# A two-layer decoder trunk: layer 0 reads raw tokens, its memory attention moves between recurrence groups, values go out 512 columns at a time, and the recurrence carries a state

## The chip, the cores and the metric

One core of one Trainium2 chip runs the whole program. The metric is the device time of one execution in microseconds (us), as a median of several runs. The engines named below are TensorE (PE, with PEld for its weight loads), VectorE (DVE), ScalarE (ACT), GpSimd (POOL) and SyncE (SP), whose queue issues the DMAs. TensorE has two clock levels, 1.2 and 2.4 GHz; a profile gives the granted share of the higher one.

## The reference, cut to what is touched

512 tokens of width 1024 pass through two layers. Layer 0 mixes tokens by a gated linear recurrence (6 heads, key and value width 128), layer 1 by latent attention; in both, a 4-head cross-attention over 256 memory rows runs beside the mixer, and a gated MLP with a 3-tap convolution follows.

```python
h = rms_norm(x, mix_norm_g[0])
z = h @ hg_w_in                       # columns [q 768 | f 768 | i 768 | g 768 | memory query 256]
q = silu(q) * 128**-0.5; fg = lb + (1-lb)*sigmoid(f); k = 1-fg; logf = log(fg); v = i
# per head, over time, b = cumulative sum of logf:
#   o[t] = sum over s<=t of (q[t] . exp(b[t]-b[s]) k[s]) v[s]
#   the reference does it in chunks with a state:
state = state * exp(b_last)[..., None] + einsum('bhsk,bhsv->bhkv', k*exp(b_last-b), v)
y = rms_norm(o, onorm_g) * silu(g)
m = memory_attention(z[..., -256:], rms_norm(mem, mem_norm_g[0]), w_mem_kv[0], ...)
x = x + concatenate([y, m]) @ w_out[0]
```

## The kernel before

**Tiling.** Activations lie transposed, eight tiles of 128 channels by 512 tokens. Each matrix product runs in three matmuls (`mm3`, L173): operands are split into a high part (`whi`, `xh`, fp32r, by ACT) and a rest (`wlo`, `xl`, by DVE), and hi·hi, hi·lo and lo·hi are summed in PSUM. Weights come by DMA in chunks of up to 128x1024 (`chunk`, L220): three `raw` buffers, two `whi` and two `wlo`. `gemm` (L242) has two forms: weights stationary and 512 tokens moving, which gives 128 channels by 512 tokens; or `tokens=True`, 128 tokens stationary and the weight's columns moving. Products inside the recurrence and the attention's values are plain fp32 and not split; each such matmul leaves two records in the trace, a transpose leaves one.

**PSUM.** Eight banks: four `acc`, two `at`, two `tp`.

**Order.** Program order is a priority, not an order of issue: when the program is built, a planner lays out each engine's queue, taking whatever is ready by its own estimate, earlier instructions first. On the chip each engine then works its own queue strictly in order. So work written later fills gaps of work written earlier, as far as buffers are free.

**Layer 0 before.** First the parameters, the memory (`mt`, 2 DMAs of 512 KB), two memory weights and the tokens (`xt`, 4 DMAs) are issued on SP. The memory rows are transposed, split (`turn`, L318) and projected (`project`, L332; 48 matmuls of 512 columns). The tokens' squares give the norm, `xn` is the scaled token (L546), 32 transposes turn it (L550) and `split` writes `nh`/`nl` (L551). Memory queries (L557; 96 matmuls of 256 columns) follow, then 32 more transposes of the raw `xt` (L561) for the residual `X`, whose second half of tokens is kept reversed (L562, L563). Then both pairs of memory heads (`attend`, L398) and the recurrence.

**The recurrence** works on three groups of two heads, in the order of `SCAN` (L82): F (forget gate), Q, G (output gate), V (values, 256 columns, L621), L (`levels`, L631) and N (`finish`, L695). `levels` doubles the block length nine times: at levels 0 to 6 it multiplies keys and queries inside windows of 128 tokens (ACT copies `kp`, PE two matmuls, DVE a predicated copy into `Ad` and three multiplies, for each of two heads); levels 7 and 8 (L671 to L680) give the products between different windows, copied by ACT to `Ao`. `finish` multiplies `Ad` and `Ao` by the values (L700 to L704), then normalizes: squares, a product with ones, an inverse root of 12 small DVE instructions, four transposes, a multiply and a split. The two heads share one buffer each for `osq` and `oy`. `kq` has two buffers for each of `Dg`, `Kc` and `Qc`. Then `out_proj` (L449): two groups, each with four `acc` banks and chunks in the order [6,7] (memory heads), [0,1], [2,3], [4,5].

**Layer 1** uses the same `Memory` class, in the order `PRE` (L80), where u is `turn` and p `project`.

Of the kernel before, what the change touches and what calls it, by code (L numbers as in the profile page):

```python
# [8 lines left out]
F32 = mybir.dt.float32  # L9
# [33 lines left out]
OFF = {0: (0, 128, 384), 1: (384, 256, 256), 3: (640, 256, 128)}  # L43
# [7 lines left out]
def _span(a, n):  # L51
    return [(a, a + n)]


def _weights():
    w = {}
    w["hg_w_in"] = (("hg_w_in", 0), [
        (_span(o + 256 * b, 256), QUADS) for b in range(3) for o in (768, 0, 1536, 2304)] + [(_span(3072, 256), QUADS)])
# [21 lines left out]
PRE = "a L b n u c p m d q k r"  # L80

SCAN = "F0 Q0 G0 L0 V0 F1 Q1 L1 N0 V1 G1 F2 Q2 N1 L2 V2 G2 N2"  # L82
# [14 lines left out]
def hybrid_trunk_kernel(ctx, tc, x, mem, params, pos, wts, out, tap):  # L97
# [208 lines left out]
    class Memory:  # L306
        def __init__(self, layer, pool):
            self.layer = layer
# [4 lines left out]
        def load(self, pool):  # L313
            self.mt = [pool.tile([P, D], F32, name=f"mt{b}") for b in range(2)]
            for b in range(2):
                nc.sync.dma_start(self.mt[b], mem[b * P:(b + 1) * P, :])

        def turn(self, pool):  # L318
            self.mth = [pool.tile([P, MEM], F32R, name=f"mth{d}") for d in range(KD)]
            self.mtl = [pool.tile([P, MEM], F32R, name=f"mtl{d}") for d in range(KD)]  # L320
            for d2 in range(KD // 2):
                ps = tp_tile()
                for d in range(2):
                    for b in range(2):
                        c = (2 * d2 + d) * P
                        transpose(ps[:, d * MEM + b * P:d * MEM + (b + 1) * P], self.mt[b][:, c:c + P])
                for d in range(2):
                    k = 2 * d2 + d
                    split(self.mth[k], self.mtl[k], ps[:, d * MEM:(d + 1) * MEM],
                          scale=pcol("memg", self.layer * KD + k, 1))  # L330

        def project(self):  # L332
            self.pk = [acc_tile(), acc_tile()]
            for c, kts in enumerate(PAIRS):
                hi, lo = chunk(f"w_mem_kv{self.layer}", 0, c)
                for j, kt in enumerate(kts):
                    for b in range(2):
                        r = slice(b * P, (b + 1) * P)
                        mm3(self.pk[b], self.mth[kt][:, r], self.mtl[kt][:, r], hi[:, j, :], lo[:, j, :],
                            kt == 0, kt == KD - 1)  # L340

        def keys(self, pool):
            layer, pk = self.layer, self.pk
            kv = pool.tile([P, 2, MW], F32, name="kv")
            kvf = pool.tile([P, D], F32, name="kvf")
            mss = sm.tile([P, 2], F32, name="mss")
            for b in range(2):
                act(kvf, self.mt[b], AF.Square, accum_out=mss[:, b:b + 1])
            rm = sm.tile([P, 2], F32, name="rm")
            rsqrt(rm, mss, D)  # L350
            for b in range(2):
                act(kv[:, b, :], pk[b][:, 0:MW], AF.Identity, scale=rm[:, b:b + 1])
                act(self.v[:, b, :], pk[b][:, MW:], AF.Identity, scale=rm[:, b:b + 1])
# [3 lines left out]
            kk = pool.tile([P, 2, MW], F32, name="kk")  # L357
            act(kk, kv[:, :, 0:MW], AF.Square)
# [15 lines left out]
        def queries(self, wname, group, xh, xl, tok, slot):  # L374
            self.qm = [slot(9 + i, F32) for i in range(2)]

            def evac(t, ps):
                dst = self.qm[t // 2][:, (t % 2) * MW:(t % 2 + 1) * MW]
                if tok is None:
                    act(dst, ps, AF.Copy)  # L380
                else:
                    act(dst, ps, AF.Identity, scale=tok[:, t:t + 1])

            gemm(wname, group, xh, xl, evac, tokens=True)
# [135 lines left out]
    with ExitStack() as l0:  # L520
# [4 lines left out]
        with tc.tile_pool(name="load", bufs=1) as lp, tc.tile_pool(name="mem0", bufs=1) as mp:  # L525
            memory = Memory(0, mp)
            with tc.tile_pool(name="mkt0", bufs=1) as mk:
                nc.sync.dma_start(par[:, :48], params[:, :48])
                memory.load(mk)
                for c in range(2):  # L530
                    chunk("w_mem_kv0", 0, c, ahead=True)
                xt = [lp.tile([P, D], F32, name=f"xt{t}") for t in range(NT)]
                for t in range(NT):
                    nc.sync.dma_start(xt[t], x[t * P:(t + 1) * P, :])
                nc.sync.dma_start(par[:, 48:], params[:, 48:])
                memory.turn(mk)
                memory.project()
                xn = []
                for t in range(NT):
                    xn.append(kq.tile([P, D], F32, name="xn", tag="Kc" if t < 2 else "Qc"))  # L540
                    junk = kq.tile([P, D], F32, name="junk", tag="Dg")
                    xss = sm.tile([P, 1], F32, name="xss")
                    act(junk, xt[t], AF.Square, accum_out=xss)
                    xr = sm.tile([P, 1], F32, name="xr")
                    rsqrt(xr, xss, D)
                    ts(xn[t], xt[t], xr, None, ALU.mult)  # L546
                for d in range(KD):
                    ps = tp_tile() if d % 2 else at_tile()
                    for t in range(NT):
                        transpose(ps[:, t * P:(t + 1) * P], xn[t][:, d * P:(d + 1) * P])  # L550
                    split(nh[d], nl[d], ps, scale=pcol("mixg", d, 1))  # L551
                memory.keys(mk)
            with tc.tile_pool(name="mat", bufs=1, reuse_waits="tile") as mat:
                def slot(i, dtype, n=1):
                    return mat.tile([P, S] if n == 1 else [P, n, S], dtype, name=f"slot{i}")

                memory.queries("hg_w_in", 12, nh, nl, None, slot)  # L557
                for d in range(KD):
                    ps = tp_tile()
                    for t in range(NT):  # L560
                        transpose(ps[:, t * P:(t + 1) * P], xt[t][:, d * P:(d + 1) * P])  # L561
                    nc.vector.tensor_copy(out=X[:, d, :H], in_=ps[:, :H])  # L562
                    nc.vector.tensor_copy(out=X[:, d, H:], in_=ps[:, :H - 1:-1])  # L563
                memory.norms(slot)
                memory.attend((0, 1), slot, yh, yl)
# [27 lines left out]
        with tc.tile_pool(name="scan", bufs=1, reuse_waits="tile") as sp:  # L593
            for k in range(HH):
                yh[k] = sp.tile([P, S], F32R, name=f"yh{k}")
                yl[k] = sp.tile([P, S], F32R, name=f"yl{k}")
            def silu2(ps, dst):

                act(dst, ps, AF.Tanh, scale=0.5)
                stt(dst, dst, 1.0, ps, ALU.add, ALU.mult)  # L600

            def forget(b):
# [3 lines left out]
                def ev_f(m, ps):  # L606
                    h = 2 * b + m
                    z = kq.tile([P, S], F32, name="z")
                    act(z, ps, AF.Tanh, scale=0.5)
# [3 lines left out]
                gemm("hg_w_in", 4 * b, nh, nl, ev_f)  # L613
                return Dg, Kc

            def query(b):
                Qc = kq.tile([P, 2, S], F32, name="Qc")
                gemm("hg_w_in", 4 * b + 1, nh, nl, lambda m, ps: silu2(ps, Qc[:, m, :]))
                return Qc

            def value(b):  # L621
                V = sp.tile([P, NT, 256], F32, name="V", bufs=2)
                gemm("hg_w_in", 4 * b + 2, nh, nl, lambda t, ps: act(V[:, t, :], ps, AF.Copy), tokens=True)
                return V

            def gate(b):
                Gt = sp.tile([P, 2, S], F32, name="Gt", bufs=2)
                gemm("hg_w_in", 4 * b + 3, nh, nl, lambda m, ps: silu2(ps, Gt[:, m, :]))
                return Gt

            def levels(b, Dg, Kc, Qc):  # L631

                Ad = sp.tile([P, 2, NT, P], F32, name="Ad", bufs=2)
                Ao = [sp.tile([P, 768], F32, name=f"Ao{h}", bufs=2) for h in range(2)]
                dcur = [Dg[:, h, :] for h in range(2)]

                def put(h, sb, t, src):

                    c = OFF[sb][0] + t - OFF[sb][1]
                    act(Ao[h][:, c:c + src.free_size()], src, AF.Copy)  # L640
# [9 lines left out]
                for lv in range(9):  # L650
                    m = 1 << lv
                    for h in range(2):
                        Kf, Qf = Kc[:, h, :], Qc[:, h, :]
                        ps = at_tile()
                        if lv < 8:
                            kv, qv = blocks(Kf, m, 0), blocks(Qf, m, 1)
                        if lv < 7:
                            nb = 64 // m
                            kp = kq.tile([P, H], F32, name=f"kp{h}", bufs=1)

                            act(kp.rearrange("p (b two j) -> p b two j", two=2, j=m),
                                bass.AP(tensor=kv.tensor, offset=kv.offset,
# [393 lines left out]
```

## Time and profile before

| what | us |
|---|---|
| median of 3 runs | 1253.29 |
| lowest, highest | 1253.13, 1253.79 |
| the profiled execution's own time | 1253.92 |
| its span, first to last instruction | 1251.9 |
| PE busy, DVE busy, ACT busy | 1229.0, 754.6, 561.4 |
| mean granted clock of TensorE | 0.998 of 2.4 GHz |

Busy is the union of an engine's instructions; a matmul's end is modelled and matmuls overlap, so a matmul's price is read from the distance of two starts, not from its duration. Layer 0's mixer takes the span up to about 300 us, its MLP up to about 660, layer 1's mixer up to about 860, its MLP the rest.

### The profile page before, as it was taken

How to read it: one execution, taken by the hardware profiler on the slowest of the kernel's cores; microseconds unless marked ns; L12 is line 12 of the kernel's file. 1: busy time of each engine (PE TensorE's matmuls, PEld its weight loads, DVE VectorE, ACT ScalarE, POOL GpSimd, SP SyncE). 2: the span in 40 equal slices, each digit the busy share in tenths (PEclk: the TensorE clock that was granted, in tenths of full speed). 3: DMA queues.
4: the chain of work that ended last, by engine and by line, in shares of the span. 5: the costliest groups of instructions: out<-in, count | busy, mean ns of one | idle time of the engine just before them, and what ended most of it. 6: DMA issues, size and time to landing. Idle time of an engine off the chain costs nothing.

```text
span 1251.9 us, 15952 instructions
## 1 busy us (share of the span) xinstructions
PE 1229.0 (98%) x6100; PEld 1022.4 (82%) x6100; DVE 754.6 (60%) x1536; ACT 561.4 (45%) x978; POOL 19.3 (2%) x50
## 2 busy tenths in 40 slices
PE   6999999999999999999999999999999999999998
PEld 4879888988888888888889878777888888888887
DVE  7857575665676757651425758774666766764222
ACT  6464444433443534432325689754453444443211
POOL 6000000000000000000000000000000000000000
PEclk9999999999999999999999999999999999999999
DMA  6212212122222232322323312101223233332331
GB/s 247 70 52 58 78 52 84 51 68 101 101 92 95 100 102 88 99 99 102 101 78 116 104 49 74 35 34 63 90 84 102 85 101 101 99 96 92 116 119 51
DMA packets 31756, 110.44 MB, mean 88 GB/s; under 512 B 3777, under 2 KB 4161, under 8 KB 31681
## 3 DMA queue, kind: packets, MB, share of 16 engines
q1 hardware_dynamic: 31680, 109.43, 26.5%
q8 instruction: 48, 0.79, 0.3%
q14 instruction: 28, 0.22, 0.1%
HBM read 107.32 MB, written 2.10 MB: 87 GB/s over the span
## 4 chain that ended last, share of the span: by engine, by line
PE 92%; ACT 4%; DVE 2%; issue 1%; DMA 1%; SPq 0%; DVEq 0%; ACTq 0%
PE acc L171 63%; PE at L171 24%; PE tp L202 3%; PE tp L171 3%; ACT xl L191 1%; ACT whi L191 0%; DVE wlo L179 0%; ACT pr L191 0%; ACT kv L191 0%; DMA mt<-in_mem 0%; ACT yl L191 0%; ACT q L191 0%; ACT xh L191 0%; ACT yh L191 0%; DVE Ad L667 0%
## 5 line engine op out<-in xcount | busy, mean ns | idle before, releaser
L179 DVE TENSOR_TENSOR wlo<-raw,whi 128x1024 fp32r<-128x1024 f32 (+2 forms) x201 | 240.3, 1196 | 383.0 <-ACT whi L191 377.4
L191 ACT ACTIVATE whi<-raw 128x1024 fp32r<-128x1024 f32 (+2 forms) x201 | 208.8, 1039 | 464.8 <-PE acc L171 303.7
L171 PE MATMUL acc<-xh,whi 128*128 128x512 f32 x616 | 241.3, 392 | 0.0
L171 PE MATMUL acc<-xh,wlo 128*128 128x512 f32 x616 | 241.2, 392 | 0.0
L171 PE MATMUL acc<-xl,whi 128*128 128x512 f32 x616 | 240.9, 391 | 0.0
L171 PEld LDWEIGHTS acc<-xh,whi 128*128 128x128 f32 x616 | 115.7, 188 | 24.2 <-issue 1.0
L171 PEld LDWEIGHTS acc<-xl,whi 128*128 128x128 f32 x616 | 115.7, 188 | 23.8
L171 PEld LDWEIGHTS acc<-xh,wlo 128*128 128x128 f32 x616 | 115.7, 188 | 23.6
L182 DVE SCALAR_TENSOR_TENSOR t<-u,par,t 128x510 f32<-128x510 f32 (+1 forms) x176 | 121.6, 747 | 4.2 <-ACT t L191 4.2
L171 PE MATMUL at<-xh,wlo 128*128 128x512 f32 x232 | 90.5, 390 | 0.0
L171 PE MATMUL at<-xl,whi 128*128 128x512 f32 x232 | 90.3, 389 | 0.0
L171 PE MATMUL at<-xh,whi 128*128 128x512 f32 x232 | 90.3, 389 | 0.0
L191 ACT ACTIVATE t<-u,par 128x512 f32<-128x512 f32 x88 | 67.0, 808 | 41.7 <-DVE u L179 41.7
L171 PE MATMUL acc<-wlo,xh 128*128 128x256 f32 (+2 forms) x224 | 67.8, 303 | 1.3 <-DVE wlo L179 1.3
L171 PE MATMUL acc<-whi,xh 128*128 128x256 f32 (+2 forms) x224 | 67.9, 305 | 0.5 <-ACT xh L191 0.4
L171 PE MATMUL acc<-whi,xl 128*128 128x256 f32 (+2 forms) x224 | 67.8, 303 | 0.0
L171 PE MATMUL acc<-wlo,ah 128*128 128x512 f32 x132 | 51.4, 389 | 0.0
L171 PE MATMUL acc<-whi,ah 128*128 128x512 f32 x132 | 51.4, 389 | 0.0
L171 PE MATMUL acc<-whi,al 128*128 128x512 f32 x132 | 51.4, 389 | 0.0
L171 PEld LDWEIGHTS at<-xl,whi 128*128 128x128 f32 x232 | 43.5, 188 | 9.1
L171 PEld LDWEIGHTS at<-xh,wlo 128*128 128x128 f32 x232 | 43.6, 188 | 9.0
L171 PEld LDWEIGHTS at<-xh,whi 128*128 128x128 f32 x232 | 43.6, 188 | 9.0
(326 smaller groups left out, 2159.6 us busy)
## 6 DMA issues: line engine op xcount, KB each, us to landing
raw<-in_w_up SPq DMA_DIRECT2D x88, 512.0 KB, 3.4
raw<-in_w_down SPq DMA_DIRECT2D x44, 512.0 KB, 3.5
raw<-in_hg_w_in SPq DMA_DIRECT2D x26, 512.0 KB, 3.6
raw<-in_w_out SPq DMA_DIRECT2D x16, 512.0 KB, 3.5
raw<-in_w_mem_kv SPq DMA_DIRECT2D x8, 512.0 KB, 4.4
mt<-in_mem SPq DMA_DIRECT2D x4, 512.0 KB, 4.9
xt<-in_x SPq DMA_DIRECT2D x4, 512.0 KB, 8.0
out<-u SPq DMA_DIRECT2D x8, 256.0 KB, 2.0
```

The costliest lines, as they stand in the source:

```text
L171: nc.tensor.matmul(ps, a, b, start=start, stop=stop)
L179: nc.vector.tensor_tensor(out=o, in0=a, in1=b, op=op)
L182: nc.vector.scalar_tensor_tensor(out=o, in0=a, scalar=s, in1=b, op0=op0, op1=op1)
L191: nc.scalar.activation(out=o, in_=a, func=f, **kw)
L202: nc.tensor.transpose(out=ps, in_=src, identity=ident)
```

## The change

1. **Start.** The tokens are loaded first; parameters go on ACT's queue; the first two chunks of `hg_w_in` follow the tokens on SP. 32 transposes of the raw tokens fill all eight PSUM banks (four `acc`, two `at`, two `tp`). From these `nh`/`nl` are split with the gain, and `X` is copied, half by ACT and half by DVE. The token's inverse root `tok` is computed beside it and spread over a tile `bc`.
2. **Norm on the products.** F, Q and G multiply each PSUM tile by `bc` on DVE before the tanh; values and memory queries take `tok` as the scale of the ACT copy that they had anyway.
3. **Values.** Two products with 512 columns (values of groups 0 and 1; values of group 2 beside the memory queries), in four chunks of two row tiles, instead of three plus one with 256 columns.
4. **Order.** `SCAN` carries the memory part: Mt (load, transposes, projection), Mk (keys), Mn (norms), M0 and M1 (`attend`). `turn` becomes part of `project`, with two pairs of buffers for the turned memory instead of sixteen tiles. The memory's tiles use the places of `yh`/`yl`, which `outputs()` takes just before the first N. Layer 1 uses the same new `project`.
5. **State.** Levels 7 and 8 and `Ao` go. `levels` keeps the total decay of a window (`tot`) and returns `Kc` and `Qc`, which `finish` now reads. `states` transposes three key windows for each head, copies them by ACT, multiplies them by the values and adds up three states; `finish` multiplies these by the queries.

```diff
-PRE = "a L b n u c p m d q k r"
-SCAN = "F0 Q0 G0 L0 V0 F1 Q1 L1 N0 V1 G1 F2 Q2 N1 L2 V2 G2 N2"
+PRE = "a L b n c p m d q k r"
+SCAN = "F0 Q0 Mt V1 G0 L0 Mk Mn V0 F1 M0 Q1 L1 M1 N0 G1 F2 Q2 N1 L2 G2 N2"
...
         def project(self):
-            self.pk = [acc_tile(), acc_tile()]
+            pk = [acc_tile(), acc_tile()]
             for c, kts in enumerate(PAIRS):
...
+                th = self.place(f"mth{c % 2}", [P, 2, MEM], F32R)
+                tl = self.place(f"mtl{c % 2}", [P, 2, MEM], F32R)
...
+            xt = [lp.tile([P, D], F32, name=f"xt{t}") for t in range(NT)]
+            nc.scalar.dma_start(par[:, :48], params[:, :48])
+            for t in range(NT):
+                nc.sync.dma_start(xt[t], x[t * P:(t + 1) * P, :])
+            for c in range(2):
+                chunk("hg_w_in", 0, c, ahead=True)
+            nc.scalar.dma_start(par[:, 48:], params[:, 48:])
+            ps8 = [acc_tile() for _ in range(4)] + [at_tile() for _ in range(2)] + [tp_tile() for _ in range(2)]
+            xss = sm.tile([P, NT], F32, name="xss", bufs=1)
+            for t in range(NT):
                 for d in range(KD):
+                    transpose(ps8[d][:, t * P:(t + 1) * P], xt[t][:, d * P:(d + 1) * P])
+                junk = kq.tile([P, D], F32, name="junk", tag="Dg")
+                act(junk, xt[t], AF.Square, accum_out=xss[:, t:t + 1])
+            for d in range(KD):
+                split(nh[d], nl[d], ps8[d], scale=pcol("mixg", d, 1))
+                act(X[:, d, :H], ps8[d][:, :H], AF.Copy)
+                nc.vector.tensor_copy(out=X[:, d, H:], in_=ps8[d][:, :H - 1:-1])
+            rsqrt(tok, xss, D)
+            spread(tok, 0, bc)
...
             def silu2(ps, dst):
-                act(dst, ps, AF.Tanh, scale=0.5)
-                stt(dst, dst, 1.0, ps, ALU.add, ALU.mult)
+                z = kq.tile([P, S], F32, name="z")
+                tt(dst, ps, bc, ALU.mult)
+                act(z, dst, AF.Tanh, scale=0.5)
+                stt(dst, z, 1.0, dst, ALU.add, ALU.mult)
...
+                if g == 0:
+                    v4 = sp.tile([P, NT, 512], F32, name="v4")
+                    gemm("hg_w_in", 9, nh, nl, lambda t, ps: act(v4[:, t, :], ps, AF.Identity, scale=tok[:, t:t + 1]), tokens=True)
+                    V[0], V[1] = v4[:, :, :256], v4[:, :, 256:]
...
-                for lv in range(9):
+                for lv in range(7):
...
+            def states(b, Kc, tot, V):
+                St = sp.tile([P, 2, 3, P], F32, name="St", bufs=1)
+                for h in range(2):
+                    c = slice(h * P, (h + 1) * P)
+                    ps = at_tile()
+                    for i in range(3):
+                        w = TIME[i]
+                        transpose(ps[:, i * P:(i + 1) * P], Kc[:, h, w * P:(w + 1) * P])
+                    kt_ = kq.tile([P, 3, P], F32, name="ktok", bufs=1)
+                    act(kt_, ps[:, :3 * P].rearrange("p (i k) -> p i k", k=P), AF.Copy)
+                    up = at_tile()
+                    for i in range(3):
+                        mm(up[:, i * P:(i + 1) * P], kt_[:, i, :], V[:, TIME[i], c], True, True)
+                    act(St[:, h, 0, :], up[:, :P], AF.Copy)
+                    for i in range(1, 3):
+                        w = TIME[i]
+                        stt(St[:, h, i, :], St[:, h, i - 1, :], tot[:, h, w:w + 1], up[:, i * P:(i + 1) * P], ALU.mult, ALU.add)
+                return St
...
-                    for sb in (0, 1, 3, 2):
-                        mm(o[:, sb * P:(sb + 1) * P], V[:, sb, c], Ad[:, h, sb, :], sb == 0, sb == 2)
-                        if sb in OFF:
-                            at, t, n = OFF[sb]
-                            mm(o[:, t:t + n], V[:, sb, c], Ao[h][:, at:at + n], False, False)
+                    for i, w in enumerate(TIME):
+                        r = slice(w * P, (w + 1) * P)
+                        mm(o[:, r], V[:, w, c], Ad[:, h, w, :], i == 0, False)
+                    for i, w in enumerate(TIME[1:]):
+                        r = slice(w * P, (w + 1) * P)
+                        mm(o[:, r], St[:, h, i, :], Qc[:, h, r], False, i == 2)
...
+                    if b == 0:
+                        outputs()
+                    finish(b, *got[f"L{b}"], V[b], got[f"G{b}"])
```

## Rows read from the trace of the kernel before

**Rows 1.** the page's first part: busy time, share of the span and count.

```profile
PE 1229.0 (98%) x6100; PEld 1022.4 (82%) x6100; DVE 754.6 (60%) x1536; ACT 561.4 (45%) x978; POOL 19.3 (2%) x50
```

**Rows 2.** busy time by stretch; the columns are named in the first line.

```profile
core 0: us, PE busy (x) PEld busy (x) DVE busy (x) ACT busy (x) POOL busy (x), PEclk, DMA share, GB/s
0.00:45.30 45.30, 34.21 (x204) 28.59 (x205) 33.86 (x122) 27.09 (x48) 19.29 (x50) 1.00 0.54 195
45.30:98.00 52.70, 52.61 (x277) 38.57 (x276) 31.73 (x79) 28.75 (x64) 0.00 (x0) 1.00 0.19 61
205.00:266.00 61.00, 60.94 (x392) 54.11 (x391) 41.92 (x129) 21.59 (x42) 0.00 (x0) 1.00 0.19 58
300.00:660.00 360.00, 360.00 (x1597) 298.38 (x1596) 208.72 (x279) 139.00 (x173) 0.00 (x0) 1.00 0.29 97
660.00:860.00 200.00, 193.01 (x1108) 160.12 (x1107) 133.41 (x437) 139.40 (x369) 0.00 (x0) 0.99 0.20 63
```

**Rows 3.** timeline of PE, 256-column matmuls: start, us, engine, line, operation, tiles, count.

```profile
35.75 0.28 PE L171 MATMUL acc<-whi,xh 128*128 128x256 f32 x1
...
37.43 0.28 PE L171 MATMUL acc<-whi,xl 128*128 128x256 f32 x1
```

**Rows 4.** timeline of PE, the residual's transposes and the first forget-gate matmul.

```profile
44.52 1.04 PE L202 MATMUL tp<-ident,xt 128*128 128x128 f32 x8
45.31 0.47 PE L171 MATMUL acc<-xh,whi 128*128 128x512 f32 x1
```

**Rows 5.** timeline of PE, one head's last products of the first recurrence group.

```profile
143.94 0.81 PE L171 MATMUL tp<-Ao,V 128*128 128x384 f32 x2
144.59 0.38 PE L171 MATMUL tp<-Ad,V 128*128 128x128 f32 x2
144.81 0.60 PE L171 MATMUL tp<-Ao,V 128*128 128x256 f32 x2
145.24 0.38 PE L171 MATMUL tp<-Ad,V 128*128 128x128 f32 x2
```

**Rows 6.** timeline of PE, the kernel's beginning.

```profile
4.99 0.45 PE L202 MATMUL tp<-ident,mt 128*128 128x128 f32 x1 [4.99 <-DMA mt<-in_mem]
...
6.17 1.76 PE L202 MATMUL tp<-ident,mt 128*128 128x128 f32 x7 [0.73 <-DMA mt<-in_mem]
...
10.20 0.79 PE L171 MATMUL acc<-whi,mth 128*128 128x512 f32 x1 [2.28 <-ACT mth L191]
...
14.97 0.63 PE L171 MATMUL acc<-wlo,mth 128*128 128x512 f32 x1
15.40 0.46 PE L171 MATMUL acc<-whi,mth 128*128 128x512 f32 x1
...
16.60 0.40 PE L171 MATMUL acc<-whi,mtl 128*128 128x512 f32 x1
16.83 0.39 PE L171 MATMUL acc<-whi,mth 128*128 128x512 f32 x1
```

**Rows 7.** timeline of DVE, splits of the normed tokens.

```profile
30.98 0.74 DVE L182 SCALAR_TENSOR_TENSOR xl<-tp,par,xh 128x512 fp32r<-128x512 f32 x1
31.63 0.74 DVE L182 SCALAR_TENSOR_TENSOR xl<-at,par,xh 128x512 fp32r<-128x512 f32 x1
```

**Rows 8.** groups of DVE instructions by form, copies into the residual: count, busy, mean ns.

```profile
L562 DVE COPY X<-tp 128x256 f32<-128x256 f32 x8 | 3.4, 419 | 0.5 <-PE tp L202 0.3
```

**Rows 9.** timeline of DVE, third recurrence group and the end of its heads.

```profile
208.30 0.68 DVE L182 SCALAR_TENSOR_TENSOR Qc<-Qc,acc 128x512 f32<-128x512 f32 x1
...
234.57 1.22 DVE L179 TENSOR_TENSOR wlo<-raw,whi 128x1024 fp32r<-128x1024 f32 x1
...
250.13 0.69 DVE L179 TENSOR_TENSOR oy<-tp,Gt 128x512 f32<-128x512 f32 x1
...
257.30 0.69 DVE L179 TENSOR_TENSOR oy<-tp,Gt 128x512 f32<-128x512 f32 x1 [0.65 <-ACT osq L191]
...
264.12 0.75 DVE L182 SCALAR_TENSOR_TENSOR yl<-oy,ongh,yh 128x512 fp32r<-128x512 f32 x1 [0.79 <-ACT yh L191]
```

More of the change, by code (lines that the diff above doesn't have):

```diff
@@ L311, in __init__, with load, project @@
             self.v = pool.tile([P, 2, MW], F32, name="mv")
-        def load(self, pool):
-            self.mt = [pool.tile([P, D], F32, name=f"mt{b}") for b in range(2)]
+        def load(self):
+            self.mt = self.place("mt", [P, 2, D], F32)
             for b in range(2):
[L316 to L321, printed above, removed]
+                nc.sync.dma_start(self.mt[:, b, :], mem[b * P:(b + 1) * P, :])
+        def project(self):
+            pk = [acc_tile(), acc_tile()]
+            for c, kts in enumerate(PAIRS):
                 ps = tp_tile()
@@ L524, in hybrid_trunk_kernel @@
         yl = {k: yp.tile([P, S], F32R, name=f"yl{k}") for k in (6, 7)}
[L525 to L546, printed above, removed]
-                for d in range(KD):
[L548 to L565, printed above, removed]
@@ L693, in levels @@
-                return Ad, Ao
-            def finish(b, Ad, Ao, V, Gt):
+                        kv, qv = blocks(Kf, m, 0), blocks(Qf, m, 1)
+                        nb = 64 // m
+                        kp = kq.tile([P, H], F32, name=f"kp{h}", bufs=1)
+                        act(kp.rearrange("p (b two j) -> p b two j", two=2, j=m),
+                            bass.AP(tensor=kv.tensor, offset=kv.offset,
+                                    ap=[list(kv.ap[0]), [2 * m, P // m], [H + m, 2], [1, m]]), AF.Copy)
@@ L696, in finish @@
+            def finish(b, Ad, Kc, Qc, tot, V, Gt):
+                St = states(b, Kc, tot, V)
                 for h in range(2):
@@ L719, in hybrid_trunk_kernel @@
             for op in SCAN.split():
-                kind, b = op[0], int(op[1])
+                kind, b = op[0], op[1]
+                if kind == "M":
+                    if b == "t":
+                        memory.load()
+                        memory.project()
+                    elif b == "k":
+                        memory.keys()
+                    elif b == "n":
+                        memory.norms(slot)
+                    else:
+                        memory.attend((int(b),), slot, yh, yl)
+                    continue
+                b = int(b)
                 if kind == "F":
@@ L725, in hybrid_trunk_kernel @@
                 elif kind == "V":
-                    got[op] = value(b)
+                    value(b)
                 elif kind == "G":
@@ L845, in hybrid_trunk_kernel @@
                     "r": krot,
-                    "q": lambda: memory.queries("mla_w_in", 2, norm.h, norm.l, norm.tok, slot),
+                    "q": lambda: (memory.query_tiles(slot), gemm("mla_w_in", 2, norm.h, norm.l, lambda t, ps: memory.put_queries(t, ps, norm.tok), tokens=True)),
                 }
```

165 lines of the change are left out of this document (76 added, 89 removed).

## The prediction

> **What bounds the kernel now.** I read the page's busy shares first [rows 1]: PE is busy 98% of the span, DVE 60%, ACT 45%. A share alone proves little, since matmuls overlap, so the windows by stretch come next [rows 2]. In the MLP of layer 0 PE starts 1597 matmuls in 360.00 us, one every 0.2254 us, with nothing idle; that is the price of a 512-column matmul. From 45.3 us on the mixer of layer 0 is filled too (52.61 of 52.70 us, 60.94 of 61.00). Only two places have holes: the start (34.21 of 45.30 us) and the mixer of layer 1 (193.01 of 200.00). So a change to layer 0's mixer is worth what it takes off PE's work, plus what it does to the start, minus any new hole.
>
> **Work taken off PE.** (a) *Residual transposes.* Eight take from 44.52 to 45.31 us, 0.1 each [rows 4]. The raw tokens are now transposed once. I count the first eight with the start, below; the other 24 fall away where PE is full: -2.4 us.
>
> (b) *Values in 512 columns.* A run of 256-column matmuls starts every (37.43-35.75)/14 = 0.12 us [rows 3]. Before, three value products and the memory queries are 4 x 96 = 384 of these, 46.1 us; after, 2 x 96 = 192 of 0.2254 us [rows 2], 43.3 us. -2.8 us: two narrow matmuls cost only 6% more than one wide.
>
> (c) *State for off-diagonal blocks.* From start to start, an fp32 product takes 0.65 us for 384 columns, 0.22 for 128 and 0.43 for 256 [rows 5]. Removed per head: 384+256+128 columns with `Ao`, 1.30 us; level 7's two of 128, 0.44; level 8's two of 256, 0.86; together 2.60. Added per head: three transposes 0.3, three key-value products 0.66, three state-query products 0.66; together 1.62. Six heads: -5.9 us. The ACT copies to `Ao` (four a head) give way to two; the state's two DVE steps a head replace level 7's two multiplies. Both engines have room there.
>
> Sum of (a) to (c): -11.1 us.
>
> **The start.** Before, the first forget-gate matmul starts at 45.31 us [rows 4]. Of that, work that is only moved: 16 memory transposes 1.6, 48 projection matmuls 10.8, 96 query matmuls 11.5, four key transposes 0.4, together 24.3 us. So the start costs 45.3-24.3 = 21.0 us. After, nothing but transposes is ahead of that matmul, so its time is the start's cost. A 512 KB tile lands at 4.99 us and the next 1.18 us later [rows 6]; the fourth token tile at about 8.6. Early transposes take about 0.22 us each (seven in 1.76 us with the last one's 0.45) [rows 6], so 32 end near 12 us and the last eight begin near 10.2. Then DVE, slower than ACT here, needs for each of eight row tiles one split at 0.66 us [rows 7] and one copy of 0.42 [rows 8], 8.6 us together: near 19. The first weight's rest part, one DVE instruction of 1.22 us [rows 9], stands behind these in program order: 20.3 at the latest. If the planner finds DVE and ACT free while tokens land and slips the weight ahead, the matmuls begin near 12.5 us. I take 19, near the late end, because ACT squares tokens as they land and later-written work goes last when both are ready.
>
> To this comes the slow clock. After the memory's transposes, the matmuls from 10.20 us on stepped by 0.43 us, the 1.2 GHz level (14.97 to 15.40), and by 0.23 soon after (16.60 to 16.83) [rows 6]. 5.2 us of such steps are 12 matmuls that lose 0.2 each: 2.4 us. The new start is the same case, transposes first, then matmuls; I take 2.4, bounds 0 and 2.4. Cost 21.4 (14.9 to 22.7) against 21.0: +0.4, bounds -6.1 and +1.7. The spread of the token factors adds four transposes: +0.4.
>
> The Trainium skill, "TensorE: Matmul & The Clock Gate", Part 4, says that transposes do not count as activity that lifts the clock, which speaks against a start made of transposes. The trace agrees as far as it goes: eight transposes, and matmuls at 0.43 us behind them. If transposes did lift it and it held, the 2.4 us would go and the forecast would be 1244.
>
> **Moved memory work.** The projection no longer stalls with an empty PE, but its two pairs of turned tiles tie each chunk's splits to the matmuls two chunks back. The query product and G0 can run between. Bounds 0 and 2, taken 0.5. On SP its two loads and four weights now stand behind the weights of F0 and Q0, which PE needs first anyway; 22 us of gate products cover them.
>
> **Recurrence with less cover.** While the third group's levels run, DVE is the limit: from 208.30 to 234.57 us it does levels and the previous heads' ends, and no weight split between [rows 9]. PE lives then on weights already split, at most two chunks. Before, these are the two chunks of V2 (48 matmuls of 0.12 us each, 11.5 us in all); after, G2's two (48 of 0.2254 us, 10.8). PE's own part of levels and head ends is the other half. That is even within 1 us. But then V2's successor G2 (10.8 us) is missing as cover, and the first output chunk waits for DVE: G2's two norm multiplies, its two gate steps (0.69 each) and one weight split (1.22), about 4 us, less 2 us of state products. After this the head ends need 264.12+0.75-250.13 = 14.7 us for two heads [rows 9], and PE has three output chunks of 24 matmuls, 16.2 us: covered. The 18 new norm multiplies on DVE (0.69 each, 12 us in all) lengthen such stretches a little; where DVE is not the limit they are hidden by PE. For all three groups I take +2, bounds 0 and 8.
>
> **Layer 1** does the same work in another order in a stretch with 7.0 us of holes [rows 2]: taken 0, bounds -1 and +3.
>
> **Sum** against the profiled execution: 1253.9 - 11.1 + 0.4 + 0.4 + 0.5 + 2 + 0 = 1246.1. Its median stands 0.6 below (1253.3), which gives 1245.5; I say 1246. Low end: -11.1-6.1+0.4 and -1 = -17.8, so 1235.5; high end: -11.1+1.7+0.4+2+8+3 = +4, so 1257.3. Not all ends meet at once below, so the range begins at 1237.
>
> **Rivals.**
>
> *An early start.* Weight splits slip ahead of the token splits, and the gate products begin near 12.5 us: 6 us better, 1240. For it: before, weight parts are made early when ACT waits for data. Against: squares and splits are written earlier, and all banks turn ready together. 14%.
>
> *DVE eats the gain.* Each of the three recurrence groups leaves PE bare for some 3 us, since norm multiplies and queue order push back weight splits while only two chunks are ready: 9 us in place of 2, about 1253, no change. For it: the 26 us without a weight split [rows 9]. Against: DVE is busy only 41.92 of 61.00 us over the whole end of the recurrence [rows 2], so it can work ahead. 20%.
>
> *Slower: keys and queries kept too long.* `Kc` and `Qc` are now read by `finish`, and there are two buffers. So F2's keys cannot be written before N0 has turned its own, and N0 stands behind M1 in the order, with both needing the two `at` banks that L1 also uses. PE then has after Q1 only G1 and F2 (21.7 us) and its own parts of L1 (8) and M1. Both memory pairs took what 52.7 us hold beside three gate products (32.5) and the transposes (2.4): about 17.5 us of PE, 8.7 each, and at most 26 us of time each [rows 2]. So PE has 38 us of work against 26 (M1) + 26 (L1, like the third group's [rows 9]) = 52. The 14 us would be bare: 1260. It decides once N0's key transposes come after the end of M1 and Q2 has no bank free. Against: those transposes need nothing of M1, and the planner may take them as soon as a bank is free. 16%.
>
> *The state doesn't shorten PE*, since its short products wait for ACT and DVE between: 5.9 us lost, 1252; it is part of the second rival.
>
> **How the numbers follow.** Forecast 50% (1242 to 1250), early start 14% (1236 to 1242), DVE eats the gain 20% (1250 to 1256), kept too long 16% (1256 to 1270). The range 1237 to 1257 leaves out a little of the second and most of the last, about 18%. A measurement of this kernel tells about 0.2% from no change, 2.5 us; so faster means below 1250.8: 50+14 and 2 of the third's 20, 66%. Same: 17%. Slower: 17%.
>
> **What would show it.** Right, if the first forget-gate matmul starts at 17 to 21 us with steps of 0.43 us at first; if the value matmuls are 192 of 512 columns at 0.225 us; if PE's count of off-diagonal records is gone; and if PE has holes of 1 to 3 us near the third group. Wrong, if PE waits for more than 5 us in one place between 25 and 260 us, or if the mixer of layer 1 moves by more than 3 us.

## The result, and the profile after

The change made the kernel slower: 1264.43 us median (1261.15 to 1265.08) against 1253.26 (1253.13 to 1253.79) on the same chip, a ratio of 1.0084 [1.0069, 1.0099], 11.2 us. The forecast was 1246 and its range ended at 1257. The profiled execution took 1261.15 us, 7.2 more than that of before; the other three ran at a mean granted clock of 0.988 and 0.989 where it had 0.991, and (0.991-0.988) x 1260 = 3.8 us is the distance to them.

The page's first part, of the changed kernel (busy time, share of the span, count), answers to [rows 1]:

```profile
PE 1224.7 (97%) x5886; PEld 1010.0 (80%) x5886; DVE 760.3 (60%) x1508; ACT 564.4 (45%) x979; POOL 18.9 (1%) x50
```

PE has 214 records fewer, and still ends later. So work went, and idle time and slow time came. Windows by stretch, of the changed kernel, to be read against [rows 2]:

```profile
core 0: us, PE busy (x) PEld busy (x) DVE busy (x) ACT busy (x) POOL busy (x), PEclk, DMA share, GB/s
25.00:300.00 275.00, 267.87 (x1390) 218.44 (x1389) 182.56 (x458) 120.63 (x216) 0.00 (x0) 0.98 0.22 70
90.00:110.00 20.00, 17.61 (x103) 14.25 (x102) 18.71 (x53) 8.47 (x17) 0.00 (x0) 1.00 0.06 24
158.00:176.00 18.00, 18.00 (x106) 14.45 (x104) 17.97 (x56) 7.11 (x14) 0.00 (x0) 1.00 0.07 25
176.00:192.00 16.00, 12.65 (x52) 9.98 (x52) 10.12 (x23) 7.01 (x20) 0.00 (x0) 0.68 0.20 67
```

From 25 to 300 us PE, filled before, is now idle for 7.1 us, and from 176 to 192 its mean granted clock is 0.68. Two landmarks are used from here on, both read from the profiled execution: A, the start of the last output-projection matmul of layer 0, and B, from the last MLP matmul of layer 0 to the first output-projection matmul of layer 1, the stretch of layer 1's mixer.

| kernel | time, us | A, us | B, us |
|---|---|---|---|
| before | 1253.3 | 298.2 | 147.1 |
| after | 1264.4 | 302.1 | 150.7 |
| forecast for after | 1246 | 290.4 | 147.1 |

Layer 0 is 3.9 us later where 7.8 less was forecast (all the sum's terms but layer 1), and layer 1 takes 3.6 more where 0 was forecast.

**Where PE waits.** Timeline of PE in the changed kernel (start, us, engine, line, operation, tiles, count; in brackets the idle time before and what ended it):

```profile
106.00 0.38 PE L173 MATMUL at<-kth,yh 64*128 64x256 f32 x1
106.86 0.38 PE L173 MATMUL at<-kth,yh 64*128 64x256 f32 x1 [0.48 <-DVE Ad L669]
108.19 0.39 PE L173 MATMUL at<-ktl,yh 64*128 64x256 f32 x2 [0.94 <-DVE ktl L181]
109.32 0.50 PE L173 MATMUL acc<-wlo,xh 128*128 128x512 f32 x1 [0.75 <-DVE wlo L181]
...
177.09 0.28 PE L173 MATMUL at<-kth,yh 64*128 64x256 f32 x2
180.72 0.58 PE L173 MATMUL at<-kth,yh 64*128 64x256 f32 x1 [3.35 <-ACT yl L193]
...
185.61 1.22 PE L173 MATMUL acc<-xh,wlo 128*128 128x512 f32 x2
186.62 0.63 PE L173 MATMUL acc<-xh,whi 128*128 128x512 f32 x1
187.05 0.63 PE L173 MATMUL acc<-xl,whi 128*128 128x512 f32 x1
```

Both holes are at the end of a group's `levels`. The last wait of the first is for the rest part of a weight (`wlo`). The second is charged to the memory pair M1. No projection matmul runs there to fill it (the next starts at 185.61), and whether that is the reason is what e2 tests. After the hole PE runs at the lower clock level, 0.43 us a matmul (186.62 to 187.05). The late weights lead to DVE. Its timeline in the same kernel, weight splits and what comes before the late ones:

```profile
87.24 1.23 DVE L181 TENSOR_TENSOR wlo<-raw,whi 128x1024 fp32r<-128x1024 f32 x1 [0.15 <-ACT whi L193]
...
108.05 2.35 DVE L181 TENSOR_TENSOR wlo<-raw,whi 128x1024 fp32r<-128x1024 f32 x2
...
155.02 1.23 DVE L181 TENSOR_TENSOR wlo<-raw,whi 128x1024 fp32r<-128x1024 f32 x1 [0.17 <-ACT whi L193]
...
176.01 1.28 DVE L181 TENSOR_TENSOR Gt<-acc,rbc 128x512 f32<-128x512 f32 x2
177.41 1.29 DVE L415 TENSOR_REDUCE nm<-at 128x2 f32<-128x512 f32 x2
178.61 0.68 DVE L184 SCALAR_TENSOR_TENSOR Gt<-z,Gt 128x512 f32<-128x512 f32 x1
...
179.29 0.68 DVE L184 SCALAR_TENSOR_TENSOR Gt<-z,Gt 128x512 f32<-128x512 f32 x1
179.89 2.35 DVE L181 TENSOR_TENSOR wlo<-raw,whi 128x1024 fp32r<-128x1024 f32 x2
```

No weight is split from 87.24 to 108.05, nor from 155.02 to 179.89, while the levels fill DVE (18.71 of 20 us, 17.97 of 18). In the second case a norm multiply of two tiles, the softmax maxima and the gate steps come ahead of the split as well. For this time PE has two split chunks of 24 matmuls, 24 x 0.2254 = 5.4 us each [rows 2], and the short products of the levels and the memory heads. The kernel before has such a gap too, in the first group's levels; its DVE timeline and its window there:

```profile
98.87 1.23 DVE L179 TENSOR_TENSOR wlo<-raw,whi 128x1024 fp32r<-128x1024 f32 x1 [2.27 <-PE at L171]
...
119.50 1.22 DVE L179 TENSOR_TENSOR wlo<-raw,whi 128x1024 fp32r<-128x1024 f32 x1
```

```profile
100.00:120.00 20.00, 20.00 (x162) 19.27 (x161) 19.96 (x61) 8.71 (x20) 0.00 (x0) 1.00 0.08 27
```

There 20.6 us pass without a split (98.87 to 119.50) and PE is never idle: the two chunks and PE's other work were just enough. How little there was to spare is shown by e4.

**The start.** The changed kernel's PE timeline:

```profile
7.14 1.11 PE L204 MATMUL acc<-ident,xt 128*128 128x128 f32 x4
8.05 0.63 PE L204 MATMUL at<-ident,xt 128*128 128x128 f32 x2
...
8.83 0.60 PE L204 MATMUL acc<-ident,xt 128*128 128x128 f32 x4
9.26 0.38 PE L204 MATMUL at<-ident,xt 128*128 128x128 f32 x2
...
18.98 0.76 PE L173 MATMUL acc<-xh,whi 128*128 128x512 f32 x1 [8.12 <-DVE X L541]
...
21.25 0.63 PE L173 MATMUL acc<-xh,whi 128*128 128x512 f32 x1
21.67 0.63 PE L173 MATMUL acc<-xl,whi 128*128 128x512 f32 x1
...
22.70 0.39 PE L173 MATMUL acc<-xh,whi 128*128 128x512 f32 x1
22.93 0.40 PE L173 MATMUL acc<-xl,whi 128*128 128x512 f32 x1
```

The first gate matmul starts at 18.98 us, in steps of 0.42 to 0.43 us until 22.4. PE's wait before it ends with DVE's copy out of a PSUM bank into `X`.

### The profile page after: what moved, and what is told of

The parts are those of the page before. It is cut to its first block, busy times and chain, and to the rows that moved or that the text cites. A ratio compares the mean times of both kernels' runs of the same rounds, so it can differ in the third digit from the quotient of the medians.

```text
span 1259.1 us, 15485 instructions
## 1 busy us (share of the span) xinstructions
PE 1224.7 (97%) x5886; PEld 1010.0 (80%) x5886; DVE 760.3 (60%) x1508; ACT 564.4 (45%) x979; POOL 18.9 (1%) x50
## 3 DMA queue, kind: packets, MB, share of 16 engines
q1 hardware_dynamic: 31392, 109.00, 26.7%
## 4 chain that ended last, share of the span: by engine, by line
PE 92%; ACT 4%; DVE 2%; DMA 1%; issue 1%; SPq 0%; ACTq 0%; DVEq 0%
PE acc L173 63%; PE at L173 23%; PE tp L204 3%; PE tp L173 2%; ACT xl L193 1%; DMA xt<-in_x 1%; ACT whi L193 0%; DVE wlo L181 0%; ACT yl L193 0%; ACT pr L193 0%; ACT junk L193 0%; ACT q L193 0%; ACT kv L193 0%; ACT yh L193 0%; ACT xh L193 0%
## 5 line engine op out<-in xcount | busy, mean ns | idle before, releaser
L173 PE MATMUL acc<-wlo,xh 128*128 128x512 f32 (+3 forms) x160 | 55.6, 348 | 2.1 <-DVE wlo L181 2.1
L173 PE MATMUL acc<-whi,xl 128*128 128x512 f32 (+3 forms) x160 | 56.1, 351 | 0.0
L173 PE MATMUL acc<-whi,xh 128*128 128x512 f32 (+3 forms) x160 | 54.7, 346 | 0.0
```

The lines of the kernel that those rows point to most:

```text
L173: nc.tensor.matmul(ps, a, b, start=start, stop=stop)
```

## The experiments

Four explanations of layer 0's loss stood at the outset; the first three are the theories 1 to 3 of the expectations. **Starved weights**: in DVE-bound stretches PE outlives its two split chunks; a third chunk of split weights would cure it. **Shared banks**: L1 and M1 both need the two `at` banks, and M1 at the head of PE's queue waits for one. **Keys and queries kept too long**: `Kc` and `Qc`, now read by `finish`, hold up the next group. **More DVE work**: the 18 norm multiplies push the splits back. For layer 1 the suspect was the memory projection with its turning merged in. Times are medians with lowest and highest; ratios are to the kernel before.

### e1: the second memory pair ahead of the second group's levels

```diff
-SCAN = "F0 Q0 Mt V1 G0 L0 Mk Mn V0 F1 M0 Q1 L1 M1 N0 G1 F2 Q2 N1 L2 G2 N2"
+SCAN = "F0 Q0 Mt V1 G0 L0 Mk Mn V0 F1 M0 M1 Q1 L1 N0 G1 F2 Q2 N1 L2 G2 N2"
```

> The changed kernel with one word moved in SCAN: the second pair of memory heads (M1) runs before Q1 and L1 instead of after L1. In the changed kernel PE stands still from 177.1 to 180.7 us, its queue headed by a score of M1 that waits for an at bank, and works at the 1.2 GHz level from 179.4 to 189.6 us. Theory 1 (weights starve: while the levels of a group fill DVE no rest part of a weight is split, and PE has two chunks to live on): the levels L1 still leave PE without weights, about 2 to 4 us, but with nothing of M1 ahead in the queue; 1256 to 1260. Theory 2 (the two at banks shared by L1 and M1 are the cause): the hole and the slow clock go altogether, 1253 to 1256. Theory 3 (keys and queries held until the end of a group delay F2 and Q2): no change, 1262 to 1265.

1255.91 us (1251.16 to 1256.90), ratio 1.0013 [1.0002, 1.0025]. A falls from 302.1 to 296.1, B stays (150.8). The hole at 177 us and the slow stretch behind it are gone, the one at 107 us is not (its three waits are 0.5, 0.9 and 0.7 us again). This time lies in the range that the expectation gave to shared banks (1253 to 1256), just below that of starved weights (1256 to 1260). So M1's place matters with two chunks; it does not tell why PE has nothing else to do, and e2 decides between the two. Here the hole at 107 us has a slow stretch behind it as well: the granted clock is 0.50 from 109.50 to 112.92 us, where the changed kernel's profile has 1.00.

### e2: a third chunk of split weights

Three buffers for each half of the split weights; one raw buffer less pays for part of the space.

```diff
-    wst = ctx.enter_context(tc.tile_pool(name="wst", bufs=3))
+    wst = ctx.enter_context(tc.tile_pool(name="wst", bufs=2))
...
-        hi = wst.tile([P, 1024], F32R, name="whi", bufs=2)
-        lo = wst.tile([P, 1024], F32R, name="wlo", bufs=2)
+        hi = wst.tile([P, 1024], F32R, name="whi", bufs=3)
+        lo = wst.tile([P, 1024], F32R, name="wlo", bufs=3)
```

> The changed kernel with three buffers instead of two for the split weights (whi, wlo), and two instead of three for the raw ones, so that it fits. PE can enter a group's levels with three chunks ready (16 us of matmuls) instead of two (11 us). Theory 1 (weights starve): the holes at 106 to 109 us and 177 to 181 us shrink or go, the slow clock at 179 us with them; 1254 to 1259. Theory 2 (at banks shared by M1 and L1): no change, 1262 to 1265. Theory 3 (keys and queries held): no change.

1245.86 us (1245.53 to 1248.62), ratio 0.9944 [0.9929, 0.9959]: 18.6 us below the changed kernel, and well below the 1254 to 1259 that the expectation gave to starved weights. The two profiled executions differ by 15.3: A is 289.7, 12.5 earlier, and B 146.5, 4.2 shorter, of which layer 1's output projection gives 1.3 back. DVE's weight splits in this kernel:

```profile
87.01 1.23 DVE L181 TENSOR_TENSOR wlo<-raw,whi 128x1024 fp32r<-128x1024 f32 x1 [0.68 <-ACT whi L193]
...
109.00 2.35 DVE L181 TENSOR_TENSOR wlo<-raw,whi 128x1024 fp32r<-128x1024 f32 x2
```

and its windows:

```profile
25.00:290.00 265.00, 264.59 (x1403) 216.86 (x1402) 186.34 (x464) 123.41 (x225) 0.00 (x0) 1.00 0.23 76
...
90.00:110.00 20.00, 19.79 (x116) 16.56 (x115) 18.95 (x55) 8.08 (x17) 0.00 (x0) 1.00 0.06 21
158.00:176.00 18.00, 18.00 (x102) 13.95 (x101) 16.74 (x53) 7.23 (x14) 0.00 (x0) 1.00 0.01 1
176.00:192.00 16.00, 16.00 (x88) 11.58 (x87) 9.74 (x22) 9.97 (x26) 0.00 (x0) 1.00 0.32 99
```

The gap without a split is as long as ever, 22.0 us (87.01 to 109.00), and DVE is as full, yet PE is idle for 0.4 us from 25 to 290 and its clock stays at 1.00. Where M1's products stood bare, its PE timeline now has projection matmuls between them:

```profile
173.73 0.28 PE L173 MATMUL at<-kth,yh 64*128 64x256 f32 x2
173.95 0.50 PE L173 MATMUL acc<-xh,whi 128*128 128x512 f32 x1
...
177.25 0.39 PE L173 MATMUL acc<-xh,wlo 128*128 128x512 f32 x1
```

The place of M1 in `SCAN`, the number of `at` banks and the life of `Kc` and `Qc` are those of the changed kernel. So starved weights explain layer 0, and shared banks and keys kept too long fall as costs of their own. One reservation: with a third buffer the planner lays out the queues anew, and no run keeps the old order with the larger stock.

### e5: control, the third chunk in the kernel before

The same edit on the kernel before.

> Control: the kernel before with three buffers for the split weights and two for the raw ones, nothing else. Its PE has no hole in layer 0 after 45 us, so if the third chunk only cures starvation that the change brought, the time stays within 0.2% of before (1251 to 1256). If the third chunk is simply better everywhere, 1240 to 1248, and its gain in the changed kernel (18.6 us) says little of the change.

1251.78 us (1250.79 to 1252.61), ratio 0.9988 [0.9979, 0.9998]: 1.5 us, against 18.6 in the changed kernel. A moves by 0.4 (297.8); B shrinks by 4.1 (143.0), of which the profiled run gives 1.3 back in layer 1's output projection. B gains because the kernel before has a wait of its own there, 1.34 us for a weight split ahead of 666.24 us with a granted clock of 0.50 behind it (667.5 to 670.8); neither is left. So the gain in B is not the change's doing, and in layer 0 the third chunk is worth 0.4 us where PE is filled anyway.

### e4: state and wide values alone

The kernel before with parts 3 and 5 of the change, its start, its norm, its memory ahead of the recurrence.

```diff
-        (_span(o + 256 * b, 256), QUADS) for b in range(3) for o in (768, 0, 1536, 2304)] + [(_span(3072, 256), QUADS)])
+        (_span(o + 256 * b, 256), QUADS) for b in range(3) for o in (768, 0, 2304)] + [
+        (_span(1536, 512), PAIRS), (_span(2048, 256) + _span(3072, 256), PAIRS)])
...
-SCAN = "F0 Q0 G0 L0 V0 F1 Q1 L1 N0 V1 G1 F2 Q2 N1 L2 V2 G2 N2"
+SCAN = "F0 Q0 G0 L0 V0 F1 Q1 L1 N0 G1 F2 Q2 N1 L2 G2 N2"
...
-                for lv in range(9):
+                for lv in range(7):
```

> The kernel before with the state in place of levels 7 and 8 and with values in 512 columns (group 2's beside the memory queries), but its own start, norm and memory at the start. PE's work falls by 5.9 and 2.8 us. If the sum of PE work was right and nothing new is late: 1244 to 1245. Theory 1 (weights starve) says that the value products no longer stand behind L1 and L2, so that some of it is given back there: 1246 to 1251, with holes after the levels. Theory 3 (keys and queries held until finish): F2 waits, 1252 or more.

1250.01 us (1248.95 to 1251.48), ratio 0.9973 [0.9963, 0.9983]: 3.3 us of the 8.7 that (b) and (c) of the sum take off PE; A is 295.8, 2.4 earlier than before. Its wait for weights, a timeline of PE:

```profile
129.21 0.94 PE L172 MATMUL acc<-whi,xh 128*128 128x512 f32 x3
131.84 0.49 PE L172 MATMUL acc<-wlo,xh 128*128 128x512 f32 x1 [1.69 <-DVE wlo L180]
```

and DVE's splits around it:

```profile
110.14 1.23 DVE L180 TENSOR_TENSOR wlo<-raw,whi 128x1024 fp32r<-128x1024 f32 x1 [2.26 <-PE at L172]
130.57 2.35 DVE L180 TENSOR_TENSOR wlo<-raw,whi 128x1024 fp32r<-128x1024 f32 x2
```

The gap of 20.4 us is no longer than before's 20.6. There is no norm multiply in it and no moved memory. PE has less other work in it, and runs dry. The values stand elsewhere too, those of the third group at the start; how much of the loss is due to their place is not separated. PE's waits from 46 to 300 us come to 2.5 us, against 0.2 in the kernel before, so the trace shows less than half of the missing 5.4 us as waits.

### e9: the same with a third chunk

> The kernel before with the state and the 512-column values alone (its own start, normed tokens, memory ahead of the recurrence), and with three buffers each for split weights (raw buffers two). Without the third chunk this pair brought 3.3 us of the 8.7 that its matmuls save. Starved weights: the other 5.4 come back on top of the 1.5 that a third chunk brings in the kernel before: about 1243 (1242 to 1245). Keys and queries kept too long: the third chunk frees no Kc or Qc, so only its own 1.5 come: about 1248.5 (1247.5 to 1250).

1244.37 us (1244.19 to 1245.27), ratio 0.9932 [0.9914, 0.9949]: 8.8 us below the kernel before (1253.19 beside it), 7.3 beyond the control's 1.5. Most of the missing 5.4 us is back; 1.4 is not, and no wait over 0.6 us from 25 to 300 us shows where it went. A is 291.3, 4.5 earlier than in e4, but 1.3 of this is not the stock's: the first matmul on tokens already starts at 29.76 against 31.09 us, and the granted clock rose at 14.67 against 17.61.

### e8: without the norm multiplies

F, Q and G products go to the tanh as they are; this leaves out the token norm on these products.

```diff
-                z = kq.tile([P, S], F32, name="z")
-                tt(dst, ps, bc, ALU.mult)
-                act(z, dst, AF.Tanh, scale=0.5)
-                stt(dst, z, 1.0, dst, ALU.add, ALU.mult)
+                act(dst, ps, AF.Tanh, scale=0.5)
+                stt(dst, dst, 1.0, ps, ALU.add, ALU.mult)
...
-                    tt(z, ps, bc, ALU.mult)
-                    act(z, z, AF.Tanh, scale=0.5)
+                    act(z, ps, AF.Tanh, scale=0.5)
```

> The changed kernel without the 18 multiplies by the norm on DVE in F, Q and G (the norm of these products is left out; tanh and gate step read PSUM as in the kernel before). DVE has 12 us less to do. Theory 1 (weights starve behind DVE): the weight split after L1 comes about 1.3 us earlier and the hole at 177 us shrinks by that, perhaps enough to spare the slow clock; 1256 to 1262. If the norm on DVE is the main cause of the loss: under 1253. If it is hidden: 1263 to 1265.

1261.87 us (1258.64 to 1262.87), ratio 1.0063 [1.0047, 1.0079]: 2.6 us below the changed kernel, with ranges that overlap. The gap in DVE's splits shrinks only from 24.9 to 23.9 us (154.81 to 178.72). The hole remains, and here it ends with the weight split itself, in PE's timeline:

```profile
179.99 1.22 PE L173 MATMUL acc<-xh,wlo 128*128 128x512 f32 x2 [2.51 <-DVE wlo L181]
```

The slow stretch is longer than in the changed kernel (granted clock 0.50 from 178.97 to 192.62 us, against 179.40 to 189.64), and A is 302.7, no earlier. The multiplies lengthen the gap a little; they are not the cause.

### e3 and e6: layer 1's memory part as before

Layer 1 gets back its own `turn` with sixteen turned tiles and its order; layer 0 is that of the changed kernel (e3), or of e2 (e6).

```diff
-PRE = "a L b n c p m d q k r"
+PRE = "a L b n u c p m d q k r"
...
+        def turn(self):
+            self.mth = [pool.tile([P, MEM], F32R, name=f"mth{d}") for d in range(KD)]
+            self.mtl = [pool.tile([P, MEM], F32R, name=f"mtl{d}") for d in range(KD)]
...
-                memory = Memory(1, mp, lambda name, shape, dtype: mk.tile(shape, dtype, name=name, tag=name))
+                memory = Memory1(1, mp, mk)
```

> The changed kernel with layer 1's memory as in the kernel before (all memory tiles turned in a step of their own into sixteen tiles, then projected); layer 0 is as changed. In the changed kernel the mixer of layer 1 takes 3.6 us longer than before. If the merged turning and projecting with two pairs of buffers is the cause, the time falls by 3 to 4 us, to about 1261; if that stretch only moved because everything ahead of it was laid out in another way, it stays at 1262 to 1265.

> The changed kernel with the third split chunk and with layer 1's memory as before. With the third chunk alone it took 1245.9 us; layer 1's memory alone brought 4.4. If layer 1's loss does not depend on the third chunk: 1241 to 1243. If the third chunk already covers it: 1245 to 1247.

e3: 1260.02 us (1257.25 to 1260.25), ratio 1.0047 [1.0032, 1.0062], B 147.1, that of before. (A is 304.3 in its profile, 2.2 later than in the changed kernel with the same layer 0: here too the granted clock is 0.50 behind the hole at 107 us, from 109.82 to 113.24.) e6: 1242.15 us (1241.79 to 1242.82), ratio 0.9911 [0.9896, 0.9926], B 143.0, that of e5. So the merged projection costs 3.6 us in B with two chunks of split weights (150.7-147.1) and 3.5 with three (146.5-143.0): a cost of its own. The changed kernel's PE timeline shows it:

```profile
698.18 1.04 PE L204 MATMUL tp<-ident,cq 128*128 128x128 f32 x8
701.04 0.66 PE L204 MATMUL tp<-ident,cq 128*128 128x128 f32 x4 [1.82 <-DVE cql L184]
701.90 0.66 PE L204 MATMUL tp<-ident,mt 128*128 128x128 f32 x4 [0.20 <-DVE cql L184]
703.49 0.50 PE L173 MATMUL acc<-whi,mth 128*128 128x512 f32 x1 [0.94 <-ACT mth L193]
```

PE waits for the splits of `cq`, whose bank the next transposes need, and then for the memory's first split. In e3 the first two waits are gone, and the third is 0.7 us: there the memory's transposes come first (700.43 us), and those of `cq` are spread over 708 to 711 us among the projection's matmuls, which fill the time of its splits.

### e7: the first weight loaded and split ahead of the tokens

On e2: the first chunk of `hg_w_in` goes ahead of the tokens on SP and is split ahead of the token splits; the second is split after three row tiles in program order.

```diff
+            chunk("hg_w_in", 0, 0, ahead=True)
             for t in range(NT):
                 nc.sync.dma_start(xt[t], x[t * P:(t + 1) * P, :])
-            for c in range(2):
-                chunk("hg_w_in", 0, c, ahead=True)
+            chunk("hg_w_in", 0, 1, ahead=True)
+            ready["hg_w_in", 0, 0] = chunk("hg_w_in", 0, 0)
...
             for d in range(KD):
+                if d == 3:
+                    ready["hg_w_in", 0, 1] = chunk("hg_w_in", 0, 1)
```

> The changed kernel with the third split chunk, and with the first weight chunk of F0 loaded ahead of the tokens and split first, the second split after three row tiles. PE then need not wait from 10.6 to 19 us for the first rest part. If the start is bounded by that rest part standing behind the token splits: first gate matmul at 12 to 14 us and 4 to 6 us less than with the third chunk alone, 1240 to 1242. If the token splits themselves bound it (1.1 us a row tile against 1.36 us that PE takes), or the work after it is bounded by DVE: 0 to 2 us less.

1245.42 us (1244.87 to 1246.00), ratio 0.9936 [0.9921, 0.9951]: 0.4 below e2. The first gate matmul moves from 18.77 to 18.09 us. Behind the weight the tokens come later (ACT squares the first from 6.62 instead of 4.75 us, the last from 10.55 instead of 9.54), and DVE's first token split starts at 16.22. The weight was not what set the start. A is 1.1 us earlier than in e2; B is 1.4 longer, with a granted clock of 0.50 from 687.4 to 690.8 us that e2's profile does not have. In the changed kernel DVE's timeline shows what stands ahead of the token splits:

```profile
11.52 0.49 DVE L190 TENSOR_SCALAR rs_v<-xss 128x4 f32<-128x4 f32 x1
...
14.46 1.21 DVE L181 TENSOR_TENSOR wlo<-raw,whi 128x1024 fp32r<-128x1024 f32 x1
...
15.96 1.23 DVE L181 TENSOR_TENSOR wlo<-raw,whi 128x1024 fp32r<-128x1024 f32 x1
17.10 1.40 DVE L184 SCALAR_TENSOR_TENSOR xl<-acc,par,xh 128x512 fp32r<-128x512 f32 x2
```

From 11.52 to 15.96 DVE works on the tokens' inverse root and a weight, then on the second weight, and its first token split starts at 17.10. The start was not improved further, and whether the root placed behind the splits would help was not tried.

### e10: third chunk, layer 1 as before, early second pair

e1, e2 and e3 together.

> The changed kernel with three chunks of split weights, layer 1's memory part as in the kernel before, and the second memory pair ahead of Q1 and L1. Starved weights: the hole at 177 us that the earlier pair removed is gone already with the third chunk, so moving the pair brings nothing more: 1242 (1241 to 1243.5). The memory pair's own place (its scores heading PE's queue behind the levels) is a second cost: 1239 or below.

1242.73 us (1242.11 to 1243.62), ratio 0.9918 [0.9901, 0.9936]; e6 has 1242.15. The early pair, worth 8.5 us with two chunks, is worth nothing with three. Its place is no second cost. e6 stays the best: 11.1 us below the kernel before and 22.3 below the changed one.

## Why the prediction was wrong

**The step that failed** is the term "Recurrence with less cover", +2 with bounds 0 and 8. If all of layer 0's excess is put down to it, it was 2 + 11.7 = 13.7 by landmark A, beyond its upper bound, and the third chunk takes 12.5 of that back, where it moves A by 0.4 in the kernel before. The rows bear it out: 7.1 us of idle PE from 25 to 300 us, and a slow stretch in which 8.9 us (180.72 to 189.6, where steps fall back to 0.23) yield about half the work, some 4.5 lost; together 11.6, less e2's 0.4; 1.3 of the 12.5 is not located. Three things in that term were mis-sized.
- It looked at the third group alone [rows 9], where the previous heads' ends give PE other work, and found balance "even within 1 us". The holes came at the first and second group's levels. There PE has only its chunks and short products of the levels and of the memory heads.
- It counted two chunks as 48 matmuls, 10.8 us, against 11.5 before, and called that even. But in a stretch in balance, work taken off PE leaves PE idle while the gap in the splits stays. e4 shows it alone: 8.7 us of PE work removed, the gap unchanged, 3.3 gained; e9, the same with a stock of three, gains 7.3 beyond what the stock brings by itself.
- It had no price for the clock that falls after a hole: some 4.5 us behind the second hole.

**The rival "DVE eats the gain"** had the mechanism, weight splits that come late while only two chunks are ready, with 20% and 1253. Of the two reasons that it gave, e8 shows that the norm multiplies were not the cause. What it held against itself, that DVE is busy only 41.92 of 61 us over the end of the recurrence and can work ahead [rows 2], was a mean: in the kernel before DVE is busy for 22.66 of the first 26 us of that stretch (205 to 231) and for 19.27 of the other 35. Working ahead needs buffers, and there were two. Its price of 9 us lacked the slow clock, and layer 1.

**"Keys and queries kept too long"** was nearest in time (1260) and wrong in cause, so its nearness is luck: e2 cures the hole at M1 without freeing a key. (Its 17.5 us for the memory pairs is 17.8 by its own numbers, which changes nothing.)

**Layer 1**, taken at 0 with bounds -1 and +3, cost 3.6 in B and 4.4 in the median (e3). That it "does the same work in another order in a stretch with 7.0 us of holes" was taken as cover. The order put the memory's transposes behind those of `cq`, and so took away the work that had filled the latter's wait. The prediction had named a move of more than 3 us there as a sign that it was wrong.

**What held.** The work taken off PE: with the starving gone, A is 8.5 us earlier than before (e2), where the sum without this term's 2 us had 9.8. The start: 18.98 us with 0.43 us steps at first, forecast 19 and the same steps. That the time agrees is luck. DVE made the root and both weights before the token splits, not after, and PE then waited for the copy that freed a bank, not for all eight row tiles. Nor were the slow steps those of a clock that transposes leave low: it rose during the transposes and was 0.50 again from 15.6 to 22.3 us, in PE's wait and after it. The early start did not come. "The state doesn't shorten PE" fell with e9.

**The sum, put right** by the two landmarks: 1246.1 + 11.7 in layer 0 + 3.6 in layer 1 = 1261.4, against 1261.15 profiled. This shows only that nothing was lost elsewhere.

## What to carry to other kernels

Where two engines are in balance, work taken off the one brings only part of its price (here 3.3 of 8.7 us) until the other's stock reaches across the longest stretch in which it makes nothing: measure the longest gap between two refills (here 20 to 25 us between weight splits), multiply out what the stock is worth on the engine that eats it, and take the difference, group by group and not at one place. A deeper stock paid little before the change and much after it: 1.5 us and 18.6. A hole is priced with what the clock does after it, and reordered code in an untouched layer is priced by what stood in the waits that it leaves.

## What the runs showed of the hardware

- A stretch of transposes alone raised the clock. The 128x128 fp32 transposes from 7.14 us took 0.91 us for four, those from 8.83 took 0.43 for four, and the trace's first record of the granted clock, at 8.73 us, is the higher level. The Trainium skill, "TensorE: Matmul & The Clock Gate", Part 4, says that the higher level doesn't engage for transposes; this trace shows otherwise for fp32 ones, and the measurement decides. The level did not last: PE then waited 8.12 us, and the first gate matmuls ran at 0.43 us a step.
- One hole of 3.35 us before 180.72 was followed by matmuls at 0.43 us a step until 189.6. In the 16 us from 176 to 192 the mean granted clock was 0.68, so the hole cost about 4.5 us on top of its own length.
- The same waits do not always bring the clock down. Behind the three waits near 107 us (0.5, 0.9 and 0.7 us) the granted clock was 0.50 for 3.4 us in the profiles of e1 and e3, and 1.00 in that of the changed kernel. The kernel before and e4 both wait 1.3 us for a weight split near 666 us; the clock fell behind it in the first and not in the second (0.50 and 1.00). So what a hole costs varies.
